# Convolution with 2x2 max pooling: two row algorithms on alternate image pairs, in a hand-written order

## The chip, the cores and the metric

One core of one Trainium2 chip. The time is the device time of the kernel in microseconds; for the kernel before it is 146.98 us, the median of three runs (146.45 to 147.07). The profile is of one execution; its span, from the first to the last instruction, is 145.9 us. Engines are named as in the profile: PE is the TensorE matmul, PEld its weight load, DVE is VectorE, ACT is ScalarE, POOL is GpSimd, SP is SyncE (it only issues transfers here).

## The reference: what is computed

Sixteen images of 64 channels and 64x64 pixels, a 3x3 convolution with padding 1 to 128 channels, then the maximum over 2x2 windows. All inputs and outputs are fp32.

```python
x       # (16, 64, 64, 64)
weight  # (128, 64, 3, 3), times 0.1
x_pad = np.pad(x, ((0, 0), (0, 0), (1, 1), (1, 1)))
for kh in range(3):
    for kw in range(3):
        conv[b, co] += weight[co, ci, kh, kw] * x_pad[b, ci, kh:kh+64, kw:kw+64]
output[b, c, i, j] = np.max(conv[b, c, 2*i:2*i+2, 2*j:2*j+2])   # (16, 128, 32, 32)
```

## The kernel before

Two images form a pair: the 64 channels of one lie in partitions 0 to 63, those of the other in 64 to 127. A weight matrix for one of the nine taps is 64x128, held once in each half of the partitions. So two matmuls, one for each image, use different halves of the array and can run side by side; this text calls the two together a couple. A chunk is 8 rows of 64 pixels, which is 512 columns; nine couples add up the nine taps of a chunk in the PSUM tiles pa and pb.

```python
for k in range(K * K):                       # weights: copy twice, turn on PE, evacuate
    nc.vector.tensor_copy(out=wdup[:, 0, :], in_=src)
    nc.vector.tensor_copy(out=wdup[:, 1, :], in_=src)
    nc.tensor.transpose(wp, wdup.rearrange("a b c -> a (b c)"), ident)
    nc.scalar.copy(out=wt, in_=wp)
# ... cut ...
for p in range(B // 2):                      # 8 pairs
    nc.sync.dma_start(out=xraw_t, in_=xv[:, 0 : H // 2])      # 1 MB each
    nc.sync.dma_start(out=xraw_b, in_=xv[:, H // 2 : H])
    # ... cut: zero rows on GpSimd ...
    nc.scalar.copy(out=xpad[:, 1 : 33, :], in_=xraw_t)        # fp32 to bf16
    nc.vector.tensor_copy(out=xpad[:, 33 : H + 1, :], in_=xraw_b)
    for c in range(NCHUNK):                  # 8 chunks of 8 rows
        # ... cut: pa, pb; for each of 9 taps: mv = the shifted rows ...
                nc.tensor.matmul(oa, wk[k][0:CI, :], mv[0:CI], start=st, stop=sp)         # line 96
                nc.tensor.matmul(ob, wk[k][CI:128, :], mv[CI:128], start=st, stop=sp)     # line 97
            for half, pt in ((0, pa), (1, pb)):
                nc.scalar.copy(out=sb, in_=pv)                                            # line 107
                nc.vector.tensor_tensor(out=cm, in0=sb[:, :, 0::2], in1=sb[:, :, 1::2], op=max)   # line 109
                nc.vector.tensor_tensor(out=oacc[...], in0=cm[:, 0::2, :], in1=cm[:, 1::2, :], op=max)  # line 113
    nc.scalar.dma_start(out=out_v[..., HO * WO // 2 :], in_=oacc[...])    # 512 KB; another half after chunk 4
```

Of the kernel before, what the change touches and what calls it, by code (L numbers as in the profile page):

```python
# [1 line left out]

# [5 lines left out]


@with_exitstack
def kernel(
    ctx: ExitStack,
    tc: tile.TileContext,
    x: bass.AP,
    weight: bass.AP,
    pool_size: bass.AP,
    out: bass.AP,
):
    nc = tc.nc  # L20
    FP32 = mybir.dt.float32
    BF16 = mybir.dt.bfloat16

    B, CI, H, W = x.shape
    CO, _, K, _ = weight.shape
    assert pool_size == 2
    HP = H + 2
    WP = W + 2
    HO, WO = H // 2, W // 2

    ROWS = 8
    NCHUNK = H // ROWS

    const = ctx.enter_context(tc.tile_pool(name="const", bufs=1))
    wpsum = ctx.enter_context(tc.tile_pool(name="wpsum", bufs=2, space=bass.MemoryType.PSUM))
    psum = ctx.enter_context(tc.tile_pool(name="psum", bufs=3, space=bass.MemoryType.PSUM))
    xraw_pool = ctx.enter_context(tc.tile_pool(name="xraw_pool", bufs=2))
    xpad_pool = ctx.enter_context(tc.tile_pool(name="xpad_pool", bufs=2))
    colmax_pool = ctx.enter_context(tc.tile_pool(name="colmax_pool", bufs=8))
    oacc_pool = ctx.enter_context(tc.tile_pool(name="oacc_pool", bufs=2))  # L40

    ident = const.tile([128, 128], FP32)
    make_identity(nc, ident)

    wraw = const.tile([CO, CI * K * K], FP32)
    nc.sync.dma_start(out=wraw, in_=weight.rearrange("a b c d -> a (b c d)"))  # L46

    wk = []
    for k in range(K * K):
        wdup = const.tile([CO, 2, CI], FP32, name=f"wdup_{k}")  # L50
        src = wraw.rearrange("a (ci k) -> a k ci", k=K * K)[:, k, :]
        nc.vector.tensor_copy(out=wdup[:, 0, :], in_=src)  # L52
        nc.vector.tensor_copy(out=wdup[:, 1, :], in_=src)  # L53
        wp = wpsum.tile([128, 128], FP32, name="wpsum")
        nc.tensor.transpose(wp, wdup.rearrange("a b c -> a (b c)"), ident)  # L55
        wt = const.tile([128, CO], BF16, name=f"wt_{k}")
        nc.scalar.copy(out=wt, in_=wp)  # L57
        wk.append(wt)

    out_v = out.rearrange("b c h w -> c b (h w)")  # L60

    for p in range(B // 2):
        xv = x[2 * p : 2 * p + 2].rearrange("b c h w -> (b c) h w")
        xraw_t = xraw_pool.tile([128, H // 2, W], FP32, name="xraw_t")
        xraw_b = xraw_pool.tile([128, H // 2, W], FP32, name="xraw_b")
        nc.sync.dma_start(out=xraw_t, in_=xv[:, 0 : H // 2])
        nc.sync.dma_start(out=xraw_b, in_=xv[:, H // 2 : H])

        xpad = xpad_pool.tile([128, HP, W], BF16)
        nc.gpsimd.memset(xpad[:, 0, :], 0.0)  # L70
        nc.gpsimd.memset(xpad[:, H + 1, :], 0.0)  # L71
        nc.scalar.copy(out=xpad[:, 1 : 33, :], in_=xraw_t)  # L72
        nc.vector.tensor_copy(out=xpad[:, 33 : H + 1, :], in_=xraw_b)  # L73

        oacc = oacc_pool.tile([128, 2, HO * WO], FP32)

        for c in range(NCHUNK):
            y0 = c * ROWS
            pa = psum.tile([128, ROWS, W], FP32, name="pa")
            pb = psum.tile([128, ROWS, W], FP32, name="pb")  # L80
            korder = [1, 4, 0, 3, 6, 2, 5, 8, 7]
            for i, k in enumerate(korder):
                kh, kw = k // K, k % K
                st = i == 0
                sp = i == K * K - 1
                rows = xpad[:, y0 + kh : y0 + kh + ROWS]
                if kw == 1:
                    mv = rows.rearrange("p a b -> p (a b)")
                    oa, ob = pa, pb
                elif kw == 0:  # L90
                    mv = rows[:, :, 0 : W - 1]
                    oa, ob = pa[:, :, 1:W], pb[:, :, 1:W]
                else:
                    mv = rows[:, :, 1:W]
                    oa, ob = pa[:, :, 0 : W - 1], pb[:, :, 0 : W - 1]
                nc.tensor.matmul(oa, wk[k][0:CI, :], mv[0:CI], start=st, stop=sp)  # L96
                nc.tensor.matmul(ob, wk[k][CI:128, :], mv[CI:128], start=st, stop=sp)  # L97

            for half, pt in ((0, pa), (1, pb)):
                if half == 0 and c == 5:  # L100
                    nc.scalar.dma_start(
                        out=out_v[:, 2 * p : 2 * p + 2, 0 : HO * WO // 2],
                        in_=oacc[:, :, 0 : HO * WO // 2],
                    )
                pv = pt
                sb = colmax_pool.tile([128, ROWS, W], FP32, name=f"sb{half}")
                nc.scalar.copy(out=sb, in_=pv)  # L107
                cm = colmax_pool.tile([128, ROWS, WO], FP32, name=f"cm{half}")
                nc.vector.tensor_tensor(  # L109
                    out=cm, in0=sb[:, :, 0::2], in1=sb[:, :, 1::2],  # L110
                    op=mybir.AluOpType.max,
                )
                nc.vector.tensor_tensor(  # L113
                    out=oacc.rearrange("p b (h w) -> p b h w", h=HO)[
                        :, half, y0 // 2 : y0 // 2 + ROWS // 2, :
                    ],
                    in0=cm[:, 0::2, :],
                    in1=cm[:, 1::2, :],
                    op=mybir.AluOpType.max,
                )  # L120

        nc.scalar.dma_start(
            out=out_v[:, 2 * p : 2 * p + 2, HO * WO // 2 :],
            in_=oacc[:, :, HO * WO // 2 :],
        )


# [1 line left out]
_INS = ['x', 'weight', 'pool_size']  # L129
_OUTS = [((16, 128, 32, 32), 'float32')]  # L130
#: Inputs that are plain numbers.
_NUMBERS = {'pool_size': 2}


# [26 lines left out]
```

## Time and profile before

| | us |
|---|---|
| device time, median of 3 | 146.98 |
| span of the profiled execution | 145.9 |
| PE busy, 1161 matmuls | 131.7 |
| DVE busy | 95.2 |
| ACT busy | 86.2 |
| POOL busy | 8.6 |
| DMA, 25.64 MB | mean 176 GB/s |

A busy time is the union of the engine's instructions; matmuls overlap each other, so 131.7 us of PE is time in which some matmul was under way, and not the sum of their durations. What the rows between mean is told where the prediction reads them.

### The profile page before, as it was taken

Reading aid. Unit: us, or ns where it says so; the run is one execution under the profiler, and the core shown is the slowest. Engines: PE = TensorE matmul, PEld = TensorE weight load, DVE = VectorE, ACT = ScalarE, POOL = GpSimd, SP = SyncE. Lnnn points to the kernel's source line nnn. Section 1 sums busy time; section 2 is a strip of 40 time slices with the busy share of each in tenths; the row PEclk is TensorE's granted clock in tenths of the full one; section 3 lists DMA queues with packets and bytes.
Section 4 is the critical chain, followed back from the end, with each engine's and each line's share of the span. In section 5 each row is a group of like instructions: output and inputs, shape, how many; then the busy total and the mean of one; then the engine's idle time right before and its main releaser. Section 6 shows DMA issues by size and latency. Waiting matters only on the chain.

```text
span 145.9 us, 3022 instructions
## 1 busy us (share of the span) xinstructions
PE 131.7 (90%) x1161; PEld 58.0 (40%) x1161; DVE 95.2 (65%) x282; ACT 86.2 (59%) x146; POOL 8.6 (6%) x22
## 2 busy tenths in 40 slices
PE   0159999999999999999999999999999999999930
PEld 0023344444444444444444444444444444444410
DVE  0630287686768685878679676867686858586770
ACT  3174644578555955597367755695559555463640
POOL 2000000030001200030003000300002000000000
PEclk9999999999999999999999999999999999999997
DMA  5999995308960598139840994030302112030303
GB/s 164 409 427 427 395 332 231 144 2 236 384 247 3 133 344 334 57 63 284 369 152 16 259 408 184 7 146 0 144 4 84 60 67 81 13 131 4 144 0 144
DMA packets 6813, 25.64 MB, mean 176 GB/s; under 512 B 528, under 2 KB 528, under 8 KB 4752
## 3 DMA queue, kind: packets, MB, share of 16 engines
q1 hardware_dynamic: 2448, 17.07, 32.3%
q10 hardware_dynamic: 4352, 8.39, 15.1%
q8 instruction: 9, 0.15, 0.4%
q14 instruction: 4, 0.03, 0.1%
HBM read 17.07 MB, written 8.39 MB: 175 GB/s over the span
## 4 chain that ended last, share of the span: by engine, by line
PE 90%; DMA 4%; ACT 2%; DVE 1%; SPq 0%; issue 0%; ACTq 0%
PE pa L96 86%; DMA xraw_t<-in_x_dram 4%; PE pb L97 2%; PE wpsum L55 2%; ACT xpad L72 1%; DVE cm L109 1%; ACT sb L107 0%; DVE oacc L113 0%; SPq L46 0%; ACT wt L57 0%; ACTq L107 0%
## 5 line engine op out<-in xcount | busy, mean ns | idle before, releaser
L96 PE MATMUL pa<-xpad,wt 64*128 64x504 bf16 (+1 forms) x576 | 127.6, 382 | 0.0
L97 PE MATMUL pb<-xpad,wt 64*128 64x504 bf16 (+1 forms) x576 | 127.6, 382 | 0.0
L96 PEld LDWEIGHTS <-wt 64*128 64x128 bf16 x576 | 54.8, 95 | 70.5 <-issue 3.6
L109 DVE TENSOR_TENSOR cm<-sb 128x256 f32<-128x256 f32 x128 | 53.6, 423 | 35.9 <-ACT sb L107 35.9
L107 ACT COPY sb<-pa 128x512 f32<-128x512 f32 x64 | 37.5, 585 | 46.2 <-PE pb L97 33.0
L97 PEld LDWEIGHTS <-wt 64*128 64x128 bf16 x576 | 54.8, 95 | 0.5 <-issue 0.5
L113 DVE TENSOR_TENSOR oacc<-cm 128x128 f32<-128x128 f32 x128 | 36.8, 292 | 3.9
L107 ACT COPY sb<-pb 128x512 f32<-128x512 f32 x64 | 37.9, 592 | 0.0
L72 ACT CAST xpad<-xraw_t 128x2048 bf16<-128x2048 f32 x8 | 15.3, 1909 | 4.9 <-DMA xraw_t<-in_x_dram 4.9
L70 POOL MEMSET xpad<- 128x64 bf16 x8 | 7.5, 937 | 101.2 <-DVE oacc L113 101.2
L73 DVE CAST xpad<-xraw_b 128x2048 bf16<-128x2048 f32 x8 | 9.8, 1226 | 3.4 <-DMA xraw_b<-in_x_dram 3.4
L55 PE MATMUL wpsum<-ident,wdup 128*128 128x128 f32 x9 | 3.5, 452 | 8.3 <-ACT wt L57 4.2
L71 POOL MEMSET xpad<- 128x64 bf16 x8 | 7.3, 918 | 0.0
L55 PEld LDWEIGHTS wpsum<-ident,wdup 128*128 128x128 f32 x9 | 1.6, 187 | 10.4 <-ACT wt L57 6.2
L52 DVE COPY wdup<-wraw 128x64 f32<-128x64 f32 x9 | 1.9, 209 | 3.7 <-DMA wraw<-in_weight_dram 3.7
L57 ACT CAST wt<-wpsum 128x128 bf16<-128x128 f32 x9 | 2.2, 265 | 3.1 <-PE wpsum L55 3.1
L53 DVE COPY wdup<-wraw 128x64 f32<-128x64 f32 x9 | 1.9, 208 | 0.0
L72 ACT ACT_TABLE_LOAD x1 | 1.3, 1283 | 0.7 <-PEq L142 0.7
masks.py:199 POOL TENSOR_SCALAR_AFFINE_SELECT ident<-ident 128x128 f32<-128x128 f32 x1 | 0.3, 292 | 0.0
masks.py:197 POOL MEMSET ident<- 128x128 f32 x1 | 0.2, 204 | 0.3 <-POOLq L142 0.3
L142 POOL MEMSET const-float32-0.0<- 128x1 f32 x1 | 0.1, 98 | 0.2 <-issue 0.2
L142 POOL MEMSET const-bfloat16-1.0<- 128x1 bf16 x1 | 0.1, 101 | 0.0
(2 smaller groups left out, 0.2 us busy)
## 6 DMA issues: line engine op xcount, KB each, us to landing
xraw_t<-in_x_dram SPq DMA_DIRECT2D x8, 1024.0 KB, 8.5
xraw_b<-in_x_dram SPq DMA_DIRECT2D x8, 1024.0 KB, 7.0
out_dram<-oacc ACTq DMA_DIRECT2D x16, 512.0 KB, 3.1
wraw<-in_weight_dram SPq DMA_DIRECT2D x1, 288.0 KB, 2.9
```

Of the source, the lines that this page charges most:

```text
L52: nc.vector.tensor_copy(out=wdup[:, 0, :], in_=src)
L55: nc.tensor.transpose(wp, wdup.rearrange("a b c -> a (b c)"), ident)
L57: nc.scalar.copy(out=wt, in_=wp)
L70: nc.gpsimd.memset(xpad[:, 0, :], 0.0)
L71: nc.gpsimd.memset(xpad[:, H + 1, :], 0.0)
L72: nc.scalar.copy(out=xpad[:, 1 : 33, :], in_=xraw_t)
L73: nc.vector.tensor_copy(out=xpad[:, 33 : H + 1, :], in_=xraw_b)
L96: nc.tensor.matmul(oa, wk[k][0:CI, :], mv[0:CI], start=st, stop=sp)
L97: nc.tensor.matmul(ob, wk[k][CI:128, :], mv[CI:128], start=st, stop=sp)
L107: nc.scalar.copy(out=sb, in_=pv)
L109: nc.vector.tensor_tensor(out=cm, in0=sb[:, :, 0::2], in1=sb[:, :, 1::2], op=mybir.AluOpType.max,)
L113: nc.vector.tensor_tensor(out=oacc.rearrange("p b (h w) -> p b h w", h=HO)[:, half, y0 // 2 : y0 // 2 + ROWS // 2, :], in0=cm[:, 0::2, :], ...
```

## The change: what it does and what it is for

Pooling needs the maximum of an even and an odd output row. Write x0, x1 for the two input rows of such a pair of output rows, x[-1] for the one above and x[2] for the one below, and G0, G1, G2 for the three rows of the kernel (each has three taps in a row). Then

```
even row = G0 x[-1] + G1 x0 + G2 x1          odd row = G0 x0 + G1 x1 + G2 x[2]        # 6 row products

k pairs (image pairs 0, 2, 4, 6), 5 row products, with D2 = G2 - G1, D0 = G0 - G1:
    a = D2 x1 + G0 x[-1]      b = D0 x0 + G2 x[2]      r = G1 (x0 + x1)
    max(even, odd) = max(a, b) + r

w pairs (image pairs 1, 3, 5, 7), 4 row products, with GM = (G0 - G1 + G2)/2, GP = (G0 + G1 + G2)/2:
    m2 = GM (x1 - x0)    m0 = G0 (x[-1] - x1)    m3 = G2 (x[2] - x0)    m1 = GP (x0 + x1)
    max(even, odd) = max(m2 + m0, -m2 + m3) + m1
```

The purpose is fewer matmuls: the common term is added on PE after the maximum over rows, in the accumulator. Row sums and differences are computed on DVE and GpSimd in place of whole-image casts; the k images are cast to bf16 by the transfer that loads them (issued on GpSimd), the w images stay fp32 in SBUF.

One step i treats 16 input rows (8 pooled rows) of a k pair and of a w pair; there are 16 steps. Four accumulators of two PSUM banks (128 x 1024 fp32, one half for each image) are passed round a queue. The pieces of a step, with the engine:

- PE: PA (a of k, 6 couples), PB (b of k, 6), PR (r of k, 3); P2 (m2 of w, 3), P0 (m0, 3), P3 (m3, 3), P1 (m1, 3)
- ACT: EV and ev evacuate the a tile of k and of w to SBUF (128 x 1024); SE writes -m2 into a second accumulator; OD and od copy the odd columns of the b tile (128 x 512)
- DVE: MX and mx take b = max(b, a) in PSUM (128 x 1024); CM and cm take the maximum of even and odd columns (128 x 512), and the store follows; KS and WS are the row sums; E, the row difference for P2, in steps 0 to 4 only
- GpSimd: Z and Y, the row differences for P0 and P3; E from step 5 on; the loads of the k images

Capital letters are the k pair, small ones (ev, mx, od, cm) the w pair. The order in which all this is written is fixed by hand, with the scheduler off. Every GpSimd row operation is put behind the last DVE operation on SBUF. Seven weight blocks (D2, G0, D0, G2, GM, G1, GP) are needed; six are turned on PE, four transposes each, after eight matmuls on ones that warm the array up. GP, which is used last, is turned by two transposing transfers from SBUF to SBUF. In the last step P1 runs first for one image and then for the other, so that the first can be stored while the second is computed.

The diff, cut to its core:

```diff
-    for p in range(B // 2):
-        # ... loads, casts, 8 chunks of 9 couples, evacuation, maxima as above ...
+    acc = [psum.tile([128, 2, R, W], FP32, name=f"acc_{i}") for i in range(4)]
+    free = deque(range(4))
# ... cut ...
+    def on_gpsimd(inst):
+        behind(inst, sbuf_op[0])          # the last DVE operation on SBUF
+        return inst
# ... cut ...
+    def turn_by_dma(m):                   # GP
+        lo = BLOCKS[m] - 1
+        for j in (lo, lo + 1):
+            nc.sync.dma_start_transpose(
+                out=wt[:, j : j + 3 : 2, :], in_=wq[:, j : j + 4, :].rearrange("a b c -> a (b c)")
+            )
# ... cut: taps() writes 3 couples for a row product; with only=h, the 3 matmuls of one image ...
+    def pa(i):
+        t = ta["k", i] = free.popleft()
+        taps(t, D2, step2(kx[j], 2 * q * R + 1), start=True)
+        taps(t, G0, step2(kx[j], 2 * q * R - 1), skip=0 if q == 0 else None)
+    def pb(i):
+        t = tb["k", i] = free.popleft()
+        taps(t, D0, step2(kx[j], 2 * q * R), start=True)
+        taps(t, G2, step2(kx[j], 2 * q * R + 2), skip=R - 1 if q == NQ - 1 else None)
# ... cut: pr, p2, p0, p3 likewise ...
+    def p1(i, h=None):
+        taps(tb["w", i], GP, step1(row["ws", i // NQ], i % NQ), only=h)
# ... cut ...
+    def evac(g, h=None):
+        nc.scalar.copy(out=ev[g][:, halves(h)], in_=acc[ta[g]][:, halves(h)])
+        done(g, "ev", ta, h)              # gives the tile back
+    def seed(i):
+        t = tb["w", i] = free.popleft()
+        nc.scalar.mul(acc[t], acc[ta["w", i]], -1.0)
+    def rowmax(g, h=None):
+        t = acc[tb[g]][:, halves(h)]
+        nc.vector.tensor_tensor(out=t, in0=t, in1=ev[g][:, halves(h)], op=MAX)
+    def odd(g, h=None):
+        nc.scalar.copy(out=od[g][:, halves(h)], in_=acc[tb[g]][:, halves(h), :, 1::2])
+    def colmax(g, h=None):
+        nc.vector.tensor_tensor(out=o, in0=acc[tb[g]][:, s, :, 0::2], in1=od[g][:, s], op=MAX)
+        done(g, "cm", tb, h)
+        store = nc.scalar if h == 0 else nc.sync
+        store.dma_start(out=dst[:, s], in_=src)
# ... cut ...
+    HEAD = """
+        D2 g0 D0 g2 GS g1 TD2 VD2 TG0 VG0 XO TD0 VD0 TG2 VG2 GM XE PA.0 TGM TG1 GP HGP XGP KS.0 PB.0
+        VGM E.0 WS.0 EV.0 VG1 X1 P2.0 Z.0 Y.0 SE.0 MX.0 X2 PA.1 EV.1 E.1 KS.1 WS.1 PR.0
+        P0.0 P3.0 Z.1 Y.1 OD.0 CM.0 P2.1 ev.0 PB.1 SE.1 mx.0 P0.1 P1.0 MX.1 P3.1 ev.1 od.0 PR.1
+        ... cut ...
+    """
+    STEADY = """
+        PA+0 OD-1 CM-1 P2+0 mx-1 EV+0 PB+0 SE+0 P1-1 MX+0 P0+0 od-1 P3+0 cm-1 ev+0 PR+0 KS+1
+        WS+1 Z+1 Y+1 E+2
+    """                                   # steps 4 to 12
+    TAIL = """
+        ... cut ...
+        MX.14 P1.13 od.13 cm.13 P0.14 ev.14 PR.14 KS.15 WS.15 Z.15 Y.15 OD.14 CM.14 PA.15 P2.15
+        P3.14 mx.14 EV.15.0 EV.15.1 PB.15 MX.15.1 MX.15.0 SE.15 P0.15 P3.15 ev.15.0 mx.15.0
+        ev.15.1 mx.15.1 P1.14 od.14 cm.14 PR.15 OD.15 CM.15 P1.15.0 P1.15.1
+        od.15.0 cm.15.0 od.15.1 cm.15.1
+    """
```

In the order strings T and V before a block are its turning on PE and its evacuation; XO, XE, X1, X2 cast the first rows; D2, D0, GS, GM, GP, HGP, g0, g1, g2 are the weight arithmetic. Engines run their own instructions in this order.

## The prediction

> **What bounds the kernel now.** I read the busy shares first, then the chain that ended last, then single instructions in order of time. The busy row and the chain of the page:
>
> ```profile
> PE 131.7 (90%) x1161; PEld 58.0 (40%) x1161; DVE 95.2 (65%) x282; ACT 86.2 (59%) x146; POOL 8.6 (6%) x22
> PE pa L96 86%; DMA xraw_t<-in_x_dram 4%; PE pb L97 2%; PE wpsum L55 2%; ACT xpad L72 1%; DVE cm L109 1%; ACT sb L107 0%; DVE oacc L113 0%; SPq L46 0%; ACT wt L57 0%; ACTq L107 0%
> ```
>
> A PE busy share alone would not prove a bound, because overlapping matmuls count as busy; the chain does: 88% of the span is matmuls following matmuls. How fast they follow is in the timeline. Start, duration, then the instruction, at 14 us and at 60 us:
>
> ```profile
> 14.43 0.63 PE L96 MATMUL pa<-xpad,wt 64*128 64x504 bf16 x1
> 14.86 0.63 PE L96 MATMUL pa<-xpad,wt 64*128 64x504 bf16 x1
> ...
> 60.10 0.38 PE L96 MATMUL pa<-xpad,wt 64*128 64x512 bf16 x1
> 60.10 0.38 PE L97 MATMUL pb<-xpad,wt 64*128 64x512 bf16 x1
> 60.32 0.38 PE L96 MATMUL pa<-xpad,wt 64*128 64x512 bf16 x1
> 60.32 0.38 PE L97 MATMUL pb<-xpad,wt 64*128 64x512 bf16 x1
> ```
>
> The two images of a pair run side by side (same start), and a new couple of matmuls starts every 0.22 us, whatever the single duration says. The chain repeats its chunk every 1.945 us (pieces at 90.95, 92.90, 94.84 us); that is nine couples, so one couple costs 216 ns. At 14 us the distance is still 0.43 us; it becomes 0.21 only at 18.2 us. The 64 chunks end at 140.03 us; 64 x 1.945 = 124.5, so the start (loads, weight turning, slow couples) costs what a delay of 15.5 us would. The end:
>
> ```profile
> 140.10 0.58 ACT L107 COPY sb<-pa 128x512 f32<-128x512 f32 x1 [0.87 <-PE pb L97]
> 140.58 0.59 ACT L107 COPY sb<-pb 128x512 f32<-128x512 f32 x1
> ...
> 141.84 0.29 DVE L113 TENSOR_TENSOR oacc<-cm 128x128 f32<-128x128 f32 x1
> 142.16 0.38 ACTq L122 DMA_DIRECT2D out_dram<-oacc  x1
> ```
>
> From the last matmul to the span's end at 145.9 it is 5.9 us: 2.1 of evacuation and maxima, 3.7 of the last store. So 15.5 + 124.5 + 5.9 = 145.9, and the device time of 146.98 is 1.1 above the span. DMA moves 176 GB/s on average and over 400 in its best slices; it does not bound.
>
> **What the Trainium skill says.** "TensorE: Matmul & The Clock Gate", Part 1, says that the array runs at half clock until it has been active for about 3.4 us. The trace agrees in kind: 0.43 against 0.216 us a couple, with the change 4.6 us after the couples became dense at 13.6. "VectorE: DVE Perf Modes", section on the errata, gives (N+151)/0.96 ns for an fp32 two-input operation; the trace has 423 ns for 256 elements and 292 for 128, which fits to 2 ns. Its table of tiers lets bf16 two-input operations run at twice the rate; no instruction here shows that. "GPSIMD Engine Reference", section 3, measures 4497 ns for such an operation with 2048 elements; a quarter, about 1.12 us for 512, is my estimate, unseen in this trace. "VectorE", section on the three transpose paths, gives 1309 ns for a 128x128 crossbar transpose; also unseen here.
>
> **The change part by part.** (1) *Fewer matmuls.* Max over two rows commutes with a common addend. The k pairs compute even and odd row as a common product G1(x0+x1) plus two different sums: five row products (D2, G0, D0, G2, G1), where six were needed. The w pairs use four (GM, G0, G2, GP). A step covers 8 output rows of a k pair and of a w pair: 5x3 + 4x3 = 27 couples, where before it was 36. Of 16 steps come 432 couples, where before there were 576. Steps at the image border leave out a row: 8 x 3 couples x 64 columns of 512 x 216 ns = 0.65 us less. The last product goes image by image, so three couples become six singles: 0.65 us more. Sum: 432 x 0.216 = 93.3 us, where before it was 124.5: 31.2 less.
>
> (2) *Do the other engines keep up with 27 x 0.216 = 5.83 us a step?* ACT: three evacuations of 1024 and two of 512. From 585 ns (512) and 265 (128), 0.833 ns an element: 1.01 for 1024, so 3 x 1.01 + 2 x 0.585 = 4.2 us. DVE: from 423 and 292, 1.02 ns an element: two maxima of 1024 at 1.21, two of 512 at 0.69, an fp32 row sum at 0.69, a bf16 one at half rate, 0.42: 4.9 us; in the first five steps with the row difference 5.6. GpSimd: three at 1.12 = 3.4, and two load issues in four steps. None reaches 5.83.
>
> (3) *Does the hand order leave holes?* I walked one steady step from the start of PA (0). PA to 1.30, P2 1.95, PB 3.25, the old P1 3.9, P0 4.55, P3 5.2, PR 5.83. OD reads the old b tile 0.1 to 0.7, CM 0.75 to 1.45, and PB reuses the tile at 1.95: 0.5 to spare. mx 1.45 to 2.65 before P1 at 3.25: 0.6. EV to 2.45, SE to 3.5, before P0 at 3.9: 0.4. MX 3.35 to 4.55 before PR at 5.2: 0.6. od and cm end 1.4 after P1, the next PA starts 1.95 after it: 0.5. The row operations for the next step end near 4.2. Every wait ends 0.4 us or more too early to matter, so I give steady holes only 0.5 us in all.
>
> (4) *The start.* wraw lands at 3.68 as before. D2 and D0 are two 0.36 us operations; eight warming matmuls at the slow 0.43 end near 4.2. Then 16 bf16 transposes; I guess 0.15 us each (the fp32 ones stand 0.31 apart): to 6.7. The first 17 rows: 0.85 MB with wraw, flowing from 2.2 us at 0.41 MB/us, land near 4.7; the cast is ready at 6.0. PA.0 6.7 to 8.0, GM and G1 turned to 9.2, PB.0 to 10.5, P2.0 to 11.1, PA.1 to 12.4: 21 couples, so the start is worth 12.4 - 4.5 = 7.9 us. DVE, loaded with weight arithmetic, reaches CM.0 at 14.85 where PB.1 (after 33 couples) needs it at 15.0: just in time. If the array is still slow through PA.0 and PB.0, 12 couples cost 0.21 more each: 10.5. I take the middle, 9.2.
>
> (5) *The crossbar transposes of GP.* Queued on SP when HGP is ready at about 8.4; two of 128x256, some 2.6 us each by the skill's figure, end near 14. P1.0 is their first reader, at about 17. They spare PE four transposes and DVE one evacuation in the start. On the path they add 0.
>
> (6) *The end.* After the last matmul od.15.1 must read. But ACT's own queue holds the store of image 0 before it, and that store waits for cm.15.0, which stands behind cm.14 and CM.15 on DVE. Counting from the end of PR.14: last matmul 7.8, CM.15 8.1, cm.15.0 8.5, store issue to 8.95, od.15.1 9.3, cm.15.1 9.75, then a store of 128 KB: 3.7 less 384 KB at 0.41 MB/us = 2.8 us. End 12.6 to 12.9, so 5.0 us after the last matmul, where it was 5.9.
>
> Sum: 9.2 + 93.3 + 0.5 + 5.0 = 108.0 span, + 1.1 = 109.1; I say 109.5, as unforeseen waits only add.
>
> **The rivals.** *The loop of tiles binds instead of PE.* Only four double-bank accumulators exist, and ACT, DVE and PE pass them round. For it: slack of 0.4 to 0.6 us is small beside the sum of four semaphore hops, and an evacuation from PSUM to PSUM (SE) has no model in this trace. Against: hops here take 0.04 to 0.1 us (140.01 to 140.10). If each step lost 0.4 us, 6 us more: 115.
>
> *GpSimd becomes the bound.* If a 512-element row operation took 1.7 us, and load issues 1 us each, a step would need 5.6; beyond 1.9 it binds. Its operations also read SBUF beside DVE's. At 2 us each, a step is 6.5 us: 16 x 0.7 = 11 more, 120. The profile before has only memsets there: 0.15 us at the start, but 1.2 us in mid-run, which speaks for some risk.
>
> *A cold or starved start.* The first rows come in pieces of 0.5 MB through one queue; a DMA transpose that takes 10 us in place of 3 holds later loads and P1.0. That gives 3 to 5 us: 113 to 114. *Better than thought:* array fast from PA.0 on, no holes: 106.5.
>
> **Range and chances.** PE's count is firm (93 us at a measured rate). The start may be 7.5 to 13, holes 0 to 3, the end 4.5 to 5.5; mostly not all bad together: 105.5 to 114.5. For the gain to fall under 2%, the time would have to be over 144 us, 35 above the sum; no rival comes near.
>
> **What would show it.** Right: couples 216 ns apart in mid-run, PE idle well under 3 us between 20 and 100 us, a step period of 5.83; PE chain above 80%; about 432 couples; od.15.1 starting over 1 us after the last matmul, behind the store issue. Wrong: idle time of PE charged to ACT, DVE or GpSimd in each step (tiles or GpSimd bind); couples of 0.43 us after 11 us (cold start); P1.0 waiting for a DMA; a span after the last matmul far from 5.

## Result and profile after

The changed kernel takes 108.68 us (median of 4 runs, 108.26 to 109.33); the kernel before took 146.74 beside it. The ratio is 0.740, with a 95% interval of 0.737 to 0.7435. The predicted 109.5 (105.5 to 114.5) holds it. The span of the profiled execution is 107.57 us, 38.3 less than before; its own device time is 109.33, the longest of the four.

Two rows of the page of the changed kernel, busy time by engine and the chain that ended last:

```profile
PE 99.7 (93%) x896; PEld 51.8 (48%) x896; DVE 81.8 (76%) x115; ACT 72.5 (67%) x92; POOL 60.6 (56%) x70
PE 75%; DMA 10%; DVE 8%; issue 1%; ACT 1%; SPq 0%; ACTq 0%; DVEq 0%
```

The 896 matmuls are 432 couples, 24 transposes and 8 warming matmuls. PE still carries the chain, but less of it than before (75%, where the same count gave 90%): DMA and DVE now take 18% between them. Where that is, the timelines tell. First one steady step, in start, duration, instruction (line 190 writes all row products: kx are the rows of a k pair, we, ws, wz, wy those of a w pair, for P2, P1, P0, P3; ks is PR):

```profile
54.45 1.40 PE L190 MATMUL acc<-kx,wt 64*128 64x512 bf16 x12
...
55.89 1.01 ACT L297 COPY ev<-acc 128x1024 f32<-128x1024 f32 x1 [0.63 <-PE acc L190]
...
56.93 1.01 ACT L306 ACTIVATE acc<-acc 128x1024 f32<-128x1024 f32 x1
...
57.62 0.83 PE L190 MATMUL acc<-ws,wt 64*128 64x512 bf16 x6
...
58.27 0.83 PE L190 MATMUL acc<-wz,wt 64*128 64x512 bf16 x6
...
60.21 1.48 PE L190 MATMUL acc<-kx,wt 64*128 64x512 bf16 x12
```

No PE line in it has an idle time in brackets. From PA to the next PA it is 5.76 us; a step without a border row takes 5.83 (83.39 to 89.22). SE, the second ACT line, ends at 57.94, and P0, which needs it, starts at 58.27: 0.27 us to spare once a hop of 0.06 is taken off (the time from one engine's end to the start that waits for it; 0.06 is that from SE to P0 in e9, below). From 20.98 to 94.69 us lie 342 couples, 73.4 us after the border columns are taken off, in 73.71 us. That leaves 0.3 us of holes in 74, and they lie at one place: PR.14 waits for MX.14 and starts at 94.03.

The start of the same kernel, the lines in which PE or its suppliers wait:

```profile
6.01 1.39 PE L190 MATMUL acc<-kx,wt 64*128 64x512 bf16 x12
6.70 0.33 SPq L100 DMA_DIRECT2D wx<-in_x_dram  x1
...
7.82 2.57 SPq L172 DMA_TRANSPOSE wt<-wq  x2
...
10.06 1.47 PE L190 MATMUL acc<-kx,wt 64*128 64x512 bf16 x12
...
13.51 0.69 DVE L255 TENSOR_TENSOR we<-wx 128x512 bf16<-128x512 f32 x1 [2.76 <-DMA wx<-in_x_dram]
...
14.27 0.82 PE L190 MATMUL acc<-we,wt 64*128 64x512 bf16 x6 [0.79 <-DVE we L255]
...
15.80 1.47 PE L190 MATMUL acc<-kx,wt 64*128 64x512 bf16 x12 [0.71 <-DVE o L329]
...
20.98 0.83 PE L190 MATMUL acc<-we,wt 64*128 64x512 bf16 x6
```

PA.0 starts at 6.01 with couples already 0.216 apart, and PA.1 at 10.06. Then E.1, the row difference for P2.1, stands at the head of DVE for 2.76 us. It waits for image rows whose load was issued at 6.70, before the two transposing transfers of 7.82, and landed only at 13.5. Everything behind E.1 on DVE comes late too, so PB.1 waits once more, for CM.0. The last couple before P2.1 is through at 13.30, so P2.1 (14.27) starts 0.97 late; P2.1 is through at 14.92, so PB.1 (15.80) starts 0.88 late: 1.85 us lost. The last line is P2.2, up to which starts are compared below.

The end:

```profile
101.66 0.83 PE L190 MATMUL acc<-ws,wt 64*128 64x512 bf16 x6 [0.39 <-DVE acc L310]
...
102.53 0.37 ACT L315 COPY od<-acc 128x256 f32<-128x256 f32 x1 [0.63 <-PE acc L190]
103.39 0.37 ACTq L338 DMA_DIRECT2D out_dram<-o  x1
103.80 0.37 ACT L315 COPY od<-acc 128x256 f32<-128x256 f32 x1 [0.90 <-DVE o L329]
104.21 0.42 DVE L329 TENSOR_TENSOR o<-acc,od 128x256 f32<-128x256 f32 x1 [0.85 <-ACT od L315]
```

The last product takes six matmuls, three of image 0 and then three of image 1. Their starts are 101.66, 101.67, 101.88, 101.90, 102.09 and 102.12: they ran in couples all the same. The last couple is through at 102.31, 0.216 after its start. od.15.0, the copy of image 0, starts only at 102.53, when all six are done; od.15.1 starts at 103.80 behind ACT's store; the span ends 2.94 us after the end of cm.15.1 (the last line), 5.26 after the last couple.

### The profile page after: what moved, and what is told of

Same layout as the page of the kernel before. It is cut to its first block, busy times and chain, and to the rows that moved or that the text cites. A ratio compares the mean times of both kernels' runs of the same rounds, so it can differ in the third digit from the quotient of the medians.

```text
span 107.6 us, 2335 instructions
## 1 busy us (share of the span) xinstructions
PE 99.7 (93%) x896; PEld 51.8 (48%) x896; DVE 81.8 (76%) x115; ACT 72.5 (67%) x92; POOL 60.6 (56%) x70
## 4 chain that ended last, share of the span: by engine, by line
PE 75%; DMA 10%; DVE 8%; issue 1%; ACT 1%; SPq 0%; ACTq 0%; DVEq 0%
PE acc L190 75%; DMA wx<-in_x_dram 6%; DVE acc L310 5%; DMA kfirst<-in_x_dram 4%; DVE o L329 1%; ACT od L315 1%; DVE ws L255 1%; DVE kx L345 0%; DVE wq L364 0%; DVE ks L255 0%; SPq L105 0%; ACTq L338 0%; DVE wt L167 0%; DVEq L310 0%; DVE we L255 0%
## 5 line engine op out<-in xcount | busy, mean ns | idle before, releaser
L190 PEld LDWEIGHTS <-wt 64*128 64x128 bf16 x864 | 48.7, 94 | 46.5 <-issue 2.4
L310 DVE TENSOR_TENSOR acc<-acc,ev 128x1024 f32<-128x1024 f32 (+1 forms) x34 | 39.5, 1166 | 12.0 <-PE acc L190 11.8
L190 PE MATMUL acc<-kx,wt 64*128 64x504 bf16 (+3 forms) x384 | 46.6, 373 | 0.8 <-DVE o L329 0.7
L297 ACT COPY ev<-acc 128x1024 f32<-128x1024 f32 (+1 forms) x34 | 32.6, 964 | 13.3 <-PE acc L190 11.8
L255 POOL TENSOR_TENSOR wz<-wx 128x512 bf16<-128x512 f32 x16 | 20.3, 1271 | 31.6 <-DVE ws L255 26.1
L315 ACT COPY od<-acc 128x512 f32<-128x512 f32 (+1 forms) x33 | 18.9, 574 | 12.4 <-PE acc L190 11.5
L329 DVE TENSOR_TENSOR o<-acc,od 128x512 f32<-128x512 f32 (+1 forms) x33 | 22.1, 674 | 4.2 <-ACT od L315 4.1
L255 POOL TENSOR_TENSOR wy<-wx 128x512 bf16<-128x512 f32 x16 | 20.3, 1268 | 0.0
L306 ACT ACTIVATE acc<-acc 128x1024 f32<-128x1024 f32 x16 | 16.1, 1008 | 1.8 <-PE acc L190 1.2
L255 POOL TENSOR_TENSOR we<-wx 128x512 bf16<-128x512 f32 x11 | 14.0, 1276 | 0.1
```

Source lines behind the costliest of these rows:

```text
L190: nc.tensor.matmul(dst[:, half, i0:i1, o0:o1], wt[lo : lo + CI, m0 + kw - half, :], rows(lo, i0, i1, c0, c1), start=start and kw == 1, sto ...
L255: return engine.tensor_tensor(out=row_out(name, i), in0=row_in(t, f + a, pad), in1=row_in(t, f + b, pad), op=op)
L297: nc.scalar.copy(out=ev[g][:, halves(h)], in_=acc[ta[g]][:, halves(h)])
L306: nc.scalar.mul(acc[t], acc[ta["w", i]], -1.0)
L310: nc.vector.tensor_tensor(out=t, in0=t, in1=ev[g][:, halves(h)], op=MAX)
L315: nc.scalar.copy(out=od[g][:, halves(h)], in_=acc[tb[g]][:, halves(h), :, 1::2])
```

## The experiments

Eleven variants were run, and the changed kernel once more (e5). Each ratio is to the kernel before on the same chip. Slow executions, more than 1.5% above the fastest of their kernel, are left out of medians, ranges and ratios: two of e1's six, four of e4's six, two of e6's six, and of e10's four the one that was profiled.

| run | us, median (range) | ratio, 95% |
|---|---|---|
| changed kernel | 108.68 (108.26–109.33) | 0.740 (0.737–0.7435) |
| e1 last stores on SP | 108.23 (107.44–108.55) | 0.734 (0.730–0.738) |
| e2 GP on PE | 108.63 (108.49–109.29) | 0.739 (0.736–0.742) |
| e3 no GP block | 108.12 (107.71–108.43) | 0.734 (0.731–0.7375) |
| e4 transposes later | 109.98 (109.17 and 110.79) | 0.747 (0.741–0.753) |
| e5 changed kernel again | 108.98 (108.28–109.02) | 0.738 (0.736–0.741) |
| e6 other tail order | 108.04 (107.13–108.32) | 0.732 (0.729–0.735) |
| e7 e6 and GP on PE | 107.41 (107.27–107.59) | 0.729 (0.727–0.731) |
| e8 plain order | 155.74, one run | 1.06 (to 147.44) |
| e9 without P1 | 105.15, one run | 0.717 (to 146.64) |
| e10 E on DVE | 109.12 (108.57–110.11) | 0.744 (0.738–0.750) |
| e11 no warming | 109.25 (108.9–109.64) | 0.745 (0.7405–0.7495) |
| e12 last product whole | 108.73 (108.62–109.07) | 0.741 (0.7375–0.744) |

### The hole at 13 us: e2, e3, e4

Theory: the crossbar transposes of GP hold up the load that E.1 waits for. Rival: the load is late anyway, because a load of k rows with its cast runs beside it. e2 turns GP on PE with four more transposes, as the other blocks are; e3 leaves out GP and its turning, and P1 multiplies by GM in its place, so the number of couples stays; e4 keeps the two transfers but writes them behind MX.0.

```diff
  e2   (HEAD)
-  ... TGM TG1 GP HGP XGP KS.0 PB.0 VGM E.0 ...
+  ... TGM GP TGP TG1 KS.0 PB.0 VGM VGP E.0 ...
  e3
-        taps(tb["w", i], GP, step1(row["ws", i // NQ], i % NQ), only=h)
+        taps(tb["w", i], GM, step1(row["ws", i // NQ], i % NQ), only=h)
-  ... TGM TG1 GP HGP XGP KS.0 PB.0 ...
+  ... TGM TG1 KS.0 PB.0 ...
  e4
+            behind(inst, last_max[0])       # the transposes wait for MX.0
-  ... GP HGP XGP KS.0 ... SE.0 MX.0 X2 ...
+  ... GP HGP KS.0 ... SE.0 MX.0 XGP X2 ...
```

> GP is turned by four transposes on PE and evacuated on ACT, in place of the two crossbar transposes. Theory (the crossbar transposes take the DMA engines from the second w chunk, which landed at 13.5 us): the chunk lands near 10 us, E.1 starts near 10.8 where it was 13.51, PE's two holes between 13 and 16 us (1.5 us) close, PE pays 0.4 us for the four transposes: 1.1 us less, 107.6 us. Rival (loads of the start are slow with or without them, because the k load with a cast runs beside them): the chunk still lands after 12.5 us and the time is 0.4 us more, 109.1.

> GP is neither computed nor turned; P1 uses the block GM instead (this leaves out the GP block). It shows the start without any cost of turning GP. Theory (crossbar transposes hold up the loads): E.1 near 10.8 us, no PE holes between 13 and 16 us, 1.5 us less: 107.2 us. Rival (they are hidden): within 0.2 us of 108.7.

> The same two crossbar transposes, issued only behind MX.0 (10.8 us) instead of at 7.8 us. Theory (their place in time is what costs): the second w chunk lands near 10 us as without them, E.1 starts near 10.8, but P1.0 (at about 16.3) may have to wait for GP until 17: between 0.5 and 1.2 us less than 108.7. Rival (loads are slow anyway): E.1 still after 13 us, P1.0 waits besides: 109 to 110 us.

In e3 the load lands at 11.38 us where it was 13.5, and PE has no hole: P2.2 starts at 19.17 where it was 20.98. E.1 and P2.2 in the timeline of e3:

```profile
11.40 0.69 DVE L255 TENSOR_TENSOR we<-wx 128x512 bf16<-128x512 f32 x1 [0.66 <-DMA wx<-in_x_dram]
...
19.17 0.81 PE L190 MATMUL acc<-we,wt 64*128 64x512 bf16 x6
```

How full the transfers were is in the windows of 2 us (window, its length, busy times and counts of PE, PEld, DVE, ACT and POOL, granted clock, DMA share, and last GB/s; the share adds up the times of the packets, and so it can pass 1). Of the changed kernel:

```profile
10.00:12.00 2.00, 1.95 (x20) 1.01 (x19) 0.76 (x1) 1.90 (x4) 2.00 (x3) 1.00 1.45 110
12.00:14.00 2.00, 1.48 (x14) 0.56 (x10) 0.49 (x1) 1.99 (x3) 0.43 (x1) 1.00 0.96 90
```

Of e3, the same windows:

```profile
10.00:12.00 2.00, 1.96 (x19) 1.02 (x20) 1.34 (x2) 1.90 (x3) 1.83 (x3) 1.00 0.69 196
12.00:14.00 2.00, 2.00 (x22) 1.15 (x20) 1.73 (x4) 1.97 (x3) 0.87 (x1) 1.00 0.96 215
```

With the two transposes under way the DMA share was twice as high or the same, and about half as many bytes were moved. All profiled executions agree: from issue to landing this load took 5.5 to 7.0 us in the nine with the transposes at that place, and 4.4 to 4.8 in the four without (e2, e3, e7, and e4, where they come later). The k load ran beside it in all of them, which speaks against the rival. In e2 E.1 starts at 12.23 with no wait for a transfer, and from PA.0 to P2.2 it is 13.97 us where it was 14.97, although four more transposes lie in it. But 14.97 is one of the longer starts: with the same head it was 13.8 to 15.2 in the other executions, so this gain is not shown. The time of e2, expected at 107.6, is no better than that of the changed kernel: in the profiled execution the first rows came 0.8 later (PA.0 waited 1.29 for their cast), and GP's evacuation on ACT pushed back the cast X1, for which PE waited 0.54. e4, expected to be 0.5 to 1.2 us faster, moves the harm instead of removing it. Its E.1 starts at 11.55, but the transposes are issued at 11.29 and land 6.4 to 6.9 later. The two PE lines at P1.0 in the timeline of e4:

```profile
18.20 0.39 PE L193 MATMUL acc<-ws,wt 64*128 64x512 bf16 x1 [1.66 <-DMA wt<-wq]
...
19.09 0.82 PE L193 MATMUL acc<-ws,wt 64*128 64x512 bf16 x5 [0.50 <-DMA wt<-wq]
```

The theory stands for the load: the transposes hold it up by about 2 us. By what path they do so is not shown. What this is worth in time is less certain. In e3 it is 1.8 us at P2.2 in the trace but 0.6 in the median, and in e2 the median moves by 0.05; both intervals overlap that of the changed kernel. The hole varies from execution to execution: in e5, the same kernel once more, E.1 waits 1.90 where it was 2.76, in e12 2.98. The load is issued at 6.70 only because it is written behind GM's arithmetic on DVE; whether an earlier issue alone would close the hole was not tried.

### The end: e1, e6, e12, e5

Theory: od.15.1 is late because ACT issues the store of image 0 before it, and that store waits for cm.15.0. Rival: both last stores then share SP, so moving the store gains at most 0.4. e1 moves the store to SP; e6 puts od.15.1 ahead of cm.15.0; e12 does the last product whole; e5 is the changed kernel again, for comparison on the same chip.

```diff
  e1
-        store = nc.scalar if h == 0 else nc.sync
+        store = nc.sync
  e6   (TAIL)
-        od.15.0 cm.15.0 od.15.1 cm.15.1
+        od.15.0 od.15.1 cm.15.0 cm.15.1
  e12  (TAIL)
-        ... PR.15 OD.15 CM.15 P1.15.0 P1.15.1
-        od.15.0 cm.15.0 od.15.1 cm.15.1
+        ... PR.15 OD.15 CM.15 P1.15
+        od.15 cm.15
```

> The store of image 0 of the last step is issued on SP instead of ACT, so od.15.1 no longer stands behind it in ACT's queue. Theory (ACT's queue holds the end up): od.15.1 starts right after the last matmul, near 103.0 us where it was 103.80, cm.15.1 follows cm.15.0 directly, and the span ends 0.7 to 0.8 us earlier: 106.8 span, 107.9 us. Rival (the last store waits for its turn anyway: both stores now share SP and 0.4 us of issue comes before the last one): at most 0.4 us earlier.

> The changed kernel once more, on the chip of the next three, so that differences under 1% can be read: 108.7 us, span 107.6. If the place of the hole in the start (E.1 waits for the second w chunk) is a matter of when transfers land, it should move by some tenths from execution to execution.

> The last four pieces are written od.15.0 od.15.1 cm.15.0 cm.15.1; nothing else changes (the store of image 0 stays on ACT). Theory (od.15.1 is held by cm.15.0 as well as by the store in ACT's queue, because ACT and DVE share the accumulator tile; in the run with the store on SP it still started 0.03 us after cm.15.0): cm.15.1 ends 1.4 us after the last matmul's end where it was 2.1, and the time is 0.65 us less than the kernel after on this chip. Rival (the last store's own 3.0 us is all that counts and the first store delays it): 0.2 us or less.

> The last product, its column maximum and its store are done for both images together (P1.15, od.15, cm.15, one store of 256 KB) instead of image by image. In the trace of the kernel after, the six single matmuls of P1.15 ran side by side as three couples, so going image by image gave image 0 no head start. Theory (the split costs more than it gives, as ACT waits for DVE and for the store's issue between the halves): cm.15 ends 1.35 us after the last matmul's end where it was 2.1; the last store has 128 KB more, 0.3 us; 0.4 us less than the kernel after. Rival (the split pays, as it was written to): 0.3 us or more slower.

In e1, with no store in front of it, od.15.1 still waits for DVE's cm.15.0: its line is in the timeline of e1 as

```profile
102.72 0.37 ACT L315 COPY od<-acc 128x256 f32<-128x256 f32 x1 [0.49 <-DVE o L329]
```

From the start of the last product to the end of cm.15.1 it is 2.56 us in e1 and 2.97 in the changed kernel: 0.4 gained, the rival's size, though the cause is another. The order in which the tail is written ties the second copy to the first maximum. e6 unties it. Its end, in the timeline:

```profile
100.96 0.83 PE L190 MATMUL acc<-ws,wt 64*128 64x512 bf16 x6 [0.39 <-DVE acc L310]
...
101.83 0.65 ACT L315 COPY od<-acc 128x256 f32<-128x256 f32 x2 [0.64 <-PE acc L190]
102.51 0.76 DVE L329 TENSOR_TENSOR o<-acc,od 128x256 f32<-128x256 f32 x2 [0.42 <-ACT od L315]
```

Both copies run back to back, and cm.15.1 ends 2.30 after the start of the product: 0.67 less. Of this 0.6 arrives at the span's end (5.30 from the product's start to the end, where the changed kernel and e5 have 5.91). e12 gains 0.54 there too (5.37): one copy of 512 (0.59), one maximum (0.69) and one store take less than two of each as they were ordered, so splitting the last product, as it was written, bought nothing. The medians follow e6 (108.04 against e5's 108.98, and the intervals of the two ratios don't overlap) and don't separate e12 from the changed kernel.

### A better kernel: e7

e7 joins e6 and GP on PE. So as not to load ACT, the four transposes of GP write into the free half of G1's PSUM bank, and DVE evacuates G1 and GP in one copy of 128x1024.

```diff
-        tp = acc[turned[m]][:, int(m == "G1")]...
+        tp = acc[turned[m]][:, int(m in ("G1", "GP"))]...
+        if m == "GP":
+            return lo, hi, tp[:, 512:1024]
# ... turn_out, for G1: hi += 4, src = the whole bank ...
-        ... TGM TG1 GP HGP XGP KS.0 PB.0
+        ... TGM TG1 GP HGP TGP KS.0 PB.0
-        od.15.0 cm.15.0 od.15.1 cm.15.1
+        od.15.0 od.15.1 cm.15.0 cm.15.1
```

> As the run before, and GP is turned on PE into the free half of G1's bank, with one evacuation of 128x1024 on DVE for both, so that ACT's order in the start stays as it is. Theory (the crossbar transposes delay the second w chunk by about 2 us, which costs PE about 1.5 us of holes; PE pays 0.4 for four transposes): 0.65 + 1.0 = 1.6 us less than the kernel after on this chip, 107.0 us. Rival (a start without the hole only exposes the next wait, as the equal times of the first run with GP on PE suggest): 0.65 us less, no more.

It takes 107.41 us, 1.6 less than the changed kernel beside it (e5, 108.98), with no overlap between the runs of the two. That is the best of all that were run. Against e6 (108.04) it is 0.6 less, but there the intervals overlap, so in the times the share of GP on PE is not shown by itself. The start in the timeline of e7:

```profile
9.19 0.68 DVE L172 COPY wt<-acc 128x1024 bf16<-128x1024 bf16 x1
...
11.10 1.35 DVE L260 TENSOR_TENSOR we<-wx 128x512 bf16<-128x512 f32 x1
...
13.53 0.83 PE L195 MATMUL acc<-we,wt 64*128 64x512 bf16 x6
...
19.42 0.81 PE L195 MATMUL acc<-we,wt 64*128 64x512 bf16 x6
```

E.1 starts as its rows land (11.08) with 0.1 us of idle time before it, P2.1 follows PE's own work, and P2.2 starts at 19.42, 1.56 earlier than in the changed kernel and 1.17 earlier than in e5. The end, from the last product's start, is 0.39 shorter than e5's (5.52); together that is the 1.6 between the two. Turning GP by transfer saves PE four transposes, for which PB.0 starts 0.23 later in e7 (8.12 against 7.89). Its price at P2.2 varies: in the executions with the transposes in place P2.2 starts at 19.98 to 21.44, which is 0.6 to 2.0 later than in e7.

### What the hand order is worth: e8

e8 writes steps 4 to 12 in plain order, each step's products and evacuations one after the other, without overlap of one step's w tile with the next step's k tile. The ends of the order strings before and after it are fitted to that (cut here).

```diff
-        PA+0 OD-1 CM-1 P2+0 mx-1 EV+0 PB+0 SE+0 P1-1 MX+0 P0+0 od-1 P3+0 cm-1 ev+0 PR+0 KS+1
+        PA+0 EV+0 PB+0 MX+0 PR+0 OD+0 CM+0 P2+0 SE+0 P0+0 P3+0 ev+0 mx+0 P1+0 od+0 cm+0 KS+1
```

> Steps 4 to 12 are written in plain order, k pair from PA to CM and then w pair from P2 to cm, and nothing of step i is put into step i+1 except the row operations. Same instructions, same tiles. Theory (the order is what hides the evacuations): PR waits 1.35 us for MX, P0 1.15 us for SE, P1 1.75 us for mx in each step, 4.25 us x 9 = 38 us more: 147 us, as slow as the kernel before. Rival (PE is so far the longest that order matters little): under 10 us more.

It took 155.74 us in its one run, more than the kernel before, with the same 896 matmuls as the changed kernel. The list of waits of e8 (engine and line, what it waited for, total, times, longest), and then P1, PR, P0 and P1 again in its timeline:

```profile
PE acc L190 <- DVE acc L310: 31.2, 20, 2.7
...
PE acc L190 <- ACT acc L306: 10.4, 9, 1.2
```

```profile
65.02 0.82 PE L190 MATMUL acc<-ws,wt 64*128 64x512 bf16 x6 [1.72 <-DVE acc L310]
...
69.75 0.82 PE L190 MATMUL acc<-ks,wt 64*128 64x512 bf16 x6 [1.39 <-DVE acc L310]
...
72.38 0.82 PE L190 MATMUL acc<-wz,wt 64*128 64x512 bf16 x6 [1.16 <-ACT acc L306]
...
75.58 0.82 PE L190 MATMUL acc<-ws,wt 64*128 64x512 bf16 x6 [1.72 <-DVE acc L310]
```

Its step takes 10.55 us (65.02 to 75.58) where it was 5.83: PR waits 1.39 for MX, P0 1.16 for SE, P1 1.72 for mx, 4.3 together. Most of the rest comes from the count: a matmul's record lasts 0.16 longer than the 0.216 to the next couple, and the waits count from its end, three times a step. A quarter fewer couples on PE are worth nothing if each product waits for its evacuation; the theory held, and my 147 was too low.

### How far from the next bound: e9 and e10

e9 leaves out P1, so that the output lacks the product GP(x0 + x1): three couples a step less on PE. e10 puts E on DVE in all steps, so that DVE is busy for nearly the whole of a step.

```diff
  e9
-        taps(tb["w", i], GP, step1(row["ws", i // NQ], i % NQ), only=h)
+        pass
  e10
-        if i < 5:
+        if i < N:
```

> P1 is left out in all 16 steps (this leaves out the product GP(x0+x1) of the w pairs): 3 of 27 couples a step, 48 couples, 10.4 us of PE at 0.216 us. Nothing else changes. Theory (PE bounds every steady step and all other engines and tiles have slack): a step takes 5.18 us, the whole about 10 us less: span 97 to 98. Rival (the loop of the four accumulators, or DVE with 4.95 us a step, is nearly the bound): half of it or less, span 102 or more.

> The row difference E stays on DVE in all steps (before: from step 5 on GpSimd). DVE then has 4.95 + 0.68 = 5.63 us of work in a step of 5.83. Theory (PE bounds and DVE's slack of 0.4 to 0.6 us at each of its waits is real but used up by 0.68): between 0 and 3 us more, 108.8 to 112. Rival (slack is in truth large): no change within 0.3 us. Rival (each wait in the loop is passed on): 0.7 us in each of 11 steps, 8 us more.

e9 leaves out 48 couples, 10.4 us, and its span is 103.35, 4.2 less than that of the changed kernel. It is one run, on a chip on which the changed kernel itself was not run. One step in the timeline of e9:

```profile
53.46 1.01 ACT L297 COPY ev<-acc 128x1024 f32<-128x1024 f32 x1 [0.63 <-PE acc L190]
...
54.50 1.01 ACT L306 ACTIVATE acc<-acc 128x1024 f32<-128x1024 f32 x1
...
55.57 0.82 PE L190 MATMUL acc<-wz,wt 64*128 64x512 bf16 x6 [0.20 <-ACT acc L306]
...
57.52 1.46 PE L190 MATMUL acc<-kx,wt 64*128 64x512 bf16 x12
```

PA (52.03 to EV's start 1.43), EV 1.04 with its hop, SE 1.07 with its hop, then P0, P3 and PR in 1.95: 5.49 us, and that is the step. It is a serial loop over PE and ACT, and in the changed kernel it is hidden by 0.27 us only: 5.76 less 5.49 is the slack that SE left there. So PE bounds the changed kernel by about 5%, and my expectation for e9 forgot a slack that the prediction had found to be the smallest; its rival, that the loop of the tiles is nearly the bound, was right.

e10 leaves the steady step as it was (54.29 to 60.04, from one P3 to the next: 5.75), with DVE busy 26.6 of the 30 us from 40 to 70 where it was 23.8. So DVE had more slack there than I expected. Its time, 109.12 with an interval that overlaps the changed kernel's, shows no difference. While DVE does E, GpSimd's operation beside it takes 1.51 us (mean of 16) where it takes 1.27 in the changed kernel.

### The warming: e11

e11 leaves out the eight matmuls on ones, and issues the first load of a w image at once.

```diff
-    for n in range(8):
+    for n in range(0):
+    wload(0)
```

> The eight matmuls on ones are left out; the first w chunk, which was issued behind the fourth of them at 2.7 us, is issued at once behind kfirst. Theory (they bring the array to full clock before PA.0): PA.0 and PB.0 run at 0.43 us a couple, full clock only after 9 us or later, PE reaches P2.2 about 2 us later; 110.5 us. Rival (the start is bounded by the landing of the first rows and by DVE, so slow couples hide in holes): under 0.6 us more.

PA.0 then starts at 6.15, takes 2.58 us in place of 1.39, and the granted clock becomes full only at 8.78 (5.78 in the changed kernel); PB.0 starts at 9.25 where it was 7.89. But at P2.1 (14.66 against 14.27) little is left, and P2.2 starts at 20.55, no later than in the changed kernel (20.98) and in e5 (20.59): the slow couples fill the hole in which PE would have waited for E.1. The time is 0.3 to 0.6 more, inside the intervals. So in this kernel the hole hides what warming gives; in e7, which has no hole, it might show, which was not run.

## Why the prediction was right, step by step

The total was right by sums that held and, by luck, errors in the start that cancelled. Before and after, in the prediction's own terms:

| term | before | predicted | measured |
|---|---|---|---|
| start is worth | 15.5 | 9.2 | 8.75 |
| couples | 124.5 | 93.3 | 92.7 |
| holes | 0 | 0.5 | 0.87 |
| last couple to end | 5.9 | 5.0 | 5.26 |
| span | 145.9 | 108.0 | 107.6 |

The measured start is 20.98 (P2.2) less the 12.23 us of the 57 couples before it. The measured column ends the couples 0.216 after the last start; the prediction ended those of the kernel before with the last record. Counted alike, the kernel before has 15.3 for the start and 6.1 for the end. The step from span to device time was wrong: the prediction added 1.1, which set a median against the span of another execution. In the runs that have both it is 1.7 to 1.9 (109.33 and 107.57 here). That error, too, was covered, by the 0.4 added for unforeseen waits and by a span predicted 0.4 too long.

**(1) Fewer matmuls: right.** 432 couples at 216 ns. The 0.65 us added for the last product's singles did not come: they ran as couples. It is the whole of the 0.6 between 93.3 and 92.7. The saving of the couples, 31.8 us, is 83% of the gain of 38.3; counted alike, the start gives 6.6 and the end 0.8, and the holes take 0.9.

**(2) The other engines: right in sum.** ACT 4.21 us a step (1.01 twice, 1.01 for SE from PSUM to PSUM, 0.59 twice) for 4.2; DVE 4.94 for 4.9 (1.23, 0.69, 0.69, and 0.42 for the bf16 row sum). The bf16 row sum was reckoned at twice the rate after the Trainium skill, "VectorE: DVE Perf Modes", section on the perf-mode tier table; 417 ns against 684 for the fp32 one agrees. GpSimd 1.27 us an operation, not the 1.12 of the estimate: 3.8 a step for 3.4, with the same consequence.

**(3) The hand order: right, with a finer slack.** The walk named P0 behind SE as the smallest slack, at 0.4; it is 0.27, shown by the timeline and, from the other side, by e9. Steady holes of 0.3 come in at one place, MX.14. The walk did not go through the tail, where P1.15 waits 0.39 for mx.15.1.

**(4) The start: right in size, wrong in its parts.** Transposes took 0.10 us each, not 0.15 (the fp32 ones before, read as 0.31 apart, stand 0.24 to 0.27 apart), and PA.1 started at 10.06 where 11.1 was written: 1.05 less. The granted clock was full from 5.78 us, before PA.0, so the 1.3 us allowed for slow couples did not come. In their place stood the hole of 1.85 us. 9.2 − 1.05 − 1.3 + 1.85 = 8.7.

**(5) The crossbar transposes: wrong.** "On the path they add 0" is the step that failed. GP itself was in time: it landed near 15, a microsecond later than written, and P1.0 started at 17.74. What was looked at was their reader alone; what they did was to hold up another transfer, the rows for E.1, by 2 us (13.49 against 11.38 in e3). The rival "a DMA transpose that holds later loads" was written down at 3 to 5 us for one that takes 10; it came in at about half that size (1.85), and the load was an earlier one.

**(6) The end: right in mechanism, 0.3 short in size.** od.15.1 started 1.49 us after the last couple, behind ACT's store, where the prediction's sum has 1.15 (8.95 less 7.8). The copy and the maximum after it took 0.83 for 0.8. The 0.34 were lost earlier: cm.15.0 was to end 0.7 after the last matmul and ended 1.05 after it (103.36). CM.15 before it on DVE ended 0.49 after the last couple where 0.3 was written, and then cm.15.0 had to wait for od.15.0, which began only at 102.53, as image 0 got no head start. That the store was the cause is half the truth: e1 shows that cm.15.0 holds od.15.1 as well, and e6 that the written order does.

**The rivals.** The loop of tiles doesn't bind, but by 0.27 us a step, and e8 shows what it is when the order is not made for it. GpSimd doesn't bind, at 3.8 of 5.8 us.

## What to carry to other kernels

When the count of the bounding engine's instructions falls, compute the serial loop through the others as well: here the work fell by a quarter and the next bound stood 5% behind. Judge a transfer that is needed late by what else is in flight beside it, and not by its own reader alone; turning a block of weights on PE cost 0.23 us, and by transfer 0.6 to 2.0 at P2.2. In a tail like this one, write all copies ahead of the first operation that waits for one of them.

## What was not expected of the hardware

- Six matmuls written as three on rows 0 to 63 and then three on rows 64 to 127 started in pairs (101.66 and 101.67, 101.88 and 101.90, 102.09 and 102.12): the second three did not wait for the first. The starts are those of the records, and the whole took 0.65 us, as three couples do. No run shows whether the array or the built program put them in that order.
- Two 128x256 bf16 transposing transfers from SBUF to SBUF occupied their issuing queue for 1.3 us each, landed 7.0 and 5.9 us after issue, and while they ran all transfers together moved 110 and 90 GB/s, against 196 and 215 without them.
- The moment at which the array reaches full clock lay between 4.05 us (e2) and 6.75 (e6) in the twelve profiled executions with warming, and at 8.78 in the one without it (e11).
- DVE's fp32 row difference takes 0.68 us alone and took 1.35 beside one of GpSimd (e7); GpSimd's took 1.51 beside one of DVE, for 1.27 (e10). The Trainium skill, "SBUF — State Buffer", section "Who interferes with whom", says that a DVE instruction with two SBUF inputs contends with a GpSimd instruction that reads SBUF; both numbers agree with it.
- Weight arithmetic with 192 elements taken 9 apart in memory costs 0.50 us on DVE, where the prediction had 0.36 for the count.
